# Evicting z at the scheduler's highest priority, and holding back the second unit's states by eight turns, in a hybrid encoder kernel

## The chip, the core and the metric

The kernel runs on one core of a Trainium2 chip. A core has a matrix engine (PE, with its weight loads listed as PEld), a vector engine (DVE), an activation engine (ACT), a general-purpose engine (POOL) and a queue engine (SP); ACT, POOL and SP also issue DMA transfers. Each engine works through its own list of instructions in order and waits on semaphores for the others. The metric is the device time of one execution in microseconds (us), lower being better.

## The reference, cut to what matters

Two layers, each a token-mixing and a channel-mixing part, on 512 tokens of 1024 channels in float32. The change lies in the token mixer, in the part that the reference calls `bidirectional_ssd` and in the gate z beside it:

```python
proj = x @ w_in
u_pool, z, xbc, dt_raw, gate_logits = jnp.split(proj, list(IN_SPLITS), axis=-1)
xbc = jax.nn.silu(dwconv_centred(xbc, ssd_conv_w, ssd_conv_b))     # width 5
xs, bm, cm = jnp.split(xbc, [SSD_INNER, SSD_INNER + gn], axis=-1)
y = bidirectional_ssd(xh, dt_raw, a_log, dt_bias, bm, cm, d_skip)
y = gated_rmsnorm(y, z, ssd_norm_g)                                # v = y * silu(z), ...

# inside ssd_scan, per direction, chunks of 128 tokens, 32 heads of 64 channels, 4 groups:
decay = jnp.exp(jnp.where(lower, seg, -jnp.inf))
scores = jnp.einsum('bclgn,bcsgn->bcgls', cc, bc)
y_diag = jnp.einsum('bcghls,bcsghp->bclghp', scores[:, :, :, None] * decay, x)
y_off = jnp.einsum('blgn,bghpn,bghl->blghp', c_c, h, jnp.exp(ac_c))
new_state = jnp.einsum('blgn,bghl,blghp->bghpn', b_c, decay_end, x_c)
h = h * jnp.exp(ac_c[..., -1])[..., None, None] + new_state
```

## The kernel before, in words

**Units and jobs.** The mixer of a layer `l` works on eight units `u`, of four heads each. `unit(u)` projects the unit's x (two tiles `xp`, 512 tokens wide) and z (two banks `zp`, two chunks each) in products of three matmuls (`mm3`: high times high, high times low, low times high; lines L385 to L387; the halves `wh` and `wl` of each block of weights are made by ACT at L96 and by DVE at L97). The big products are the steady work of PE. Everything else runs as background jobs. At fixed points between the big matmuls `bg.tick()` lets the jobs go on, at most one that does something in each turn; a job says with `yield n` for how many turns it rests. So the place of each small matmul among the big ones on PE is fixed when the program is written.

**A unit's steps**, with the names in the trace: conv of x on ACT (L477) and four taps on DVE (L483), Silu on ACT (L812) gives `xc`; `xt` transposes it on PE (L818), and ACT copies it to `xtok` (L952). POOL multiplies `xtok` into `xw` (L1061, two pieces) and into `y` (L1067, `dsk`). Three matmul pairs `stp` (L1078) make the states of three chunk borders, which ACT, POOL and DVE turn into `s` (L1084, L1086, L1093). `yop` (L1105) reads them; DVE scales the result to `yo` (L1111) and POOL adds it to `y` (L1119). At the end `zs * y` on DVE (L1124).

**Heads.** For each head `decay(h)` issues a DMA of 512 KB to a tile `m` from ACT's queue (L998; three buffers, so head h+3's transfer waits for head h's matmuls), POOL masks both halves (L1003, followed by a small DMA issue from POOL, L151), ACT takes eight exponentials (L1010), DVE adds the halves (L1012) and multiplies by the scores `sct` (L1022), and PE does the 16 small matmuls `ydp` (L1029), which DVE adds to `y` (L1035). Once per two units `btp` transposes B (L818) and `scp` makes the scores (L839); their input `bt` and the unit's `xc` share two buffers.

**What sets the order.** PE follows the program. On ACT, DVE and POOL a scheduler places the instructions by priority. ACT switches its function table (`ACT_TABLE_LOAD`) whenever an exponential follows a Silu or the other way round. z's eviction is an ACT Silu from a bank to `zs` (L978).

In the trace names carry no head or unit. In layer 0, the `xw` at 120 us is `xw_1`, the `stp` at 121.7 `stp_1_1`, the `ydp` at 104.2 `ydp_3`, at 127.2 `ydp_5`, the `scp` at 144.4 `scp_1`, the `xt` at 158.5 `xt_2_1`. In the listings of the order a name is tile, layer, unit or head, part and a running number: `m0_5_1115` is head 5's decay tile of layer 0, and `xt0_2_1` is unit 2's second transpose.

Of the kernel before, what the change touches and what calls it, by code (L numbers as in the profile page):

```python
# [12 lines left out]
AF = mybir.ActivationFunctionType  # L13
# [289 lines left out]
def tile_hybrid_pool_ssd_convffn_encoder(  # L303
# [24 lines left out]
    nc = tc.nc  # L328
# [8 lines left out]
    def bank_a(name):  # L337
        return psa.tile([P, 512], F32, tag="a", name=name)

    def bank_b(name):  # L340
        return psb.tile([P, 512], F32, tag="b", name=name)
# [40 lines left out]
    def mm3(ps, ah, al, bh, bl, first, last, resumed=False):  # L382

        mm = partial(nc.tensor.matmul, ps, skip_group_check=resumed)
        mm(lhsT=ah, rhs=bh, start=first, stop=False)  # L385
        mm(lhsT=ah, rhs=bl, start=False, stop=False)  # L386
        mm(lhsT=al, rhs=bh, start=False, stop=last)  # L387
# [43 lines left out]
    def feature_tiles(name, n):  # L431

        tiles = []
        for i in range(n):
            wh, wl = ws.get()
            ps = bank_a(f"{name}{i}")
            for k in range(KD):
                mm3(ps[: wh.shape[2], :], wh[:, k, :], wl[:, k, :], xts["h"][:, k, :],
                    xts["l"][:, k, :], k == 0, k == KD - 1)
                if k % 2:  # L440
                    bg.tick()
            tiles.append(ps)
        return tiles
# [333 lines left out]
    for l in range(NL):  # L777
# [31 lines left out]
        def conv_silu(ps, ft, name, tag="cv", bufs=2):  # L809
            cv = sp.tile([P, T], F32, tag=tag, name=name, bufs=bufs)  # L810
            conv(cv, ps, xbc_taps(ft), xbc_bias(ft))
            nc.scalar.activation(cv, cv, AF.Silu)  # L812
            return cv
# [137 lines left out]
        def x_job(u, i, cv, xtok):  # L951
            nc.scalar.copy(  # L952
                xtok[:, :, i * P : (i + 1) * P], transpose_tokens(cv, f"xt{l}_{u}_{i}")
            )
            yield 1

        def unit(u):
            nm = f"{l}_{u}"
            xtok = sp.tile([P, NCH, 256], F32, tag="xtok", name=f"xtok{nm}", bufs=2)
            xjobs = []  # L960
            for i in range(2):
                (xps,) = feature_tiles(f"xp{nm}_{i}_", 1)
                cv = conv_silu(xps, 2 * u + i, f"xc{nm}_{i}")
                xjobs.append(bg.spawn(x_job(u, i, cv, xtok), 11))
            zs = sp.tile([P, NCH, 256], F32, tag="zs", name=f"zs{nm}", bufs=3)
            wz = [ws.get() for _ in range(2)]
            for cc in range(2):
                ps = bank_a(f"zp{nm}_{cc}")
                for ci in range(2):
                    c = 2 * cc + ci  # L970
                    s = slice(c * P, (c + 1) * P)
                    for k in range(KD):
                        wh, wl = wz[k // 4]
                        mm3(ps[:, ci * 256 : (ci + 1) * 256], xts["h"][:, k, s], xts["l"][:, k, s],
                            wh[:, k % 4, :], wl[:, k % 4, :], k == 0, k == KD - 1)
                        if k % 4 == 3:
                            bg.tick()
                nc.scalar.activation(  # L978
                    zs[:, 2 * cc : 2 * cc + 2, :],
                    ps.rearrange("p (c n) -> p c n", c=2), AF.Silu,  # L980
                )

            return bg.spawn(unit_job(u, xtok, zs, xjobs), 1)

# [58 lines left out]
        def unit_job(u, xtok, zs, xjobs):  # L1043
            nm = f"{l}_{u}"
            g = u // 2
            while not (dts and g in grp and all(j.done for j in xjobs)):
                yield 0
            ct, btok, sct = grp[g]
            ef, nac, wst, tot = dts["ef"], dts["nac"], dts["wst"], dts["tot"]

            def hb(tile_, c0, c1, d, h0=4 * u, nh=4):
                return tile_[:, c0:c1, d * 32 + h0 : d * 32 + h0 + nh][:, :, :, None].broadcast_to(
                    [P, c1 - c0, nh, 64]
                )

            def h4(ap):
                return ap.rearrange("p c (h q) -> p c h q", q=64)

            xw = sp.tile([P, 2, 3, 256], F32, tag="xw", name=f"xw{nm}")
            for d in range(2):  # L1060
                nc.gpsimd.tensor_tensor(  # L1061
                    h4(xw[:, d]), h4(xtok[:, d : d + 3, :]), hb(wst, d, d + 3, d), op=ALU.mult
                )
            while u and u - 1 not in zst:
                yield 0
            y = sp.tile([P, NCH, 256], F32, tag="y", name=f"y{nm}")
            nc.gpsimd.tensor_tensor(  # L1067
                h4(y), h4(xtok),
                dsk[:, None, 4 * u : 4 * u + 4][:, :, :, None].broadcast_to([P, NCH, 4, 64]),
                op=ALU.mult,  # L1070
            )
            ytiles[u] = (xtok, y)
            yield 4
            st = {}
            for i in range(1, 4):
                ps = bank_b(f"stp{nm}_{i}")
                for d, c in ((0, i - 1), (1, 4 - i)):
                    nc.tensor.matmul(  # L1078
                        ps[:, d * 256 : (d + 1) * 256], lhsT=btok[:, c, :],
                        rhs=xw[:, d, c - d, :], start=True, stop=True,  # L1080
                    )
                s_new = sp.tile([P, 512], F32, tag="st", name=f"s{nm}_{i}", bufs=3)
                if i == 1:
                    nc.scalar.copy(s_new, ps)  # L1084
                else:
                    nc.gpsimd.tensor_tensor(  # L1086
                        s_new.rearrange("p (d h q) -> p d h q", d=2, q=64),
                        st[i - 1].rearrange("p (d h q) -> p d h q", d=2, q=64),
                        tot[:, i - 2, :, 4 * u : 4 * u + 4][:, :, :, None].broadcast_to(
                            [P, 2, 4, 64]),  # L1090
                        op=ALU.mult,
                    )
                    nc.vector.tensor_tensor(s_new, s_new, ps, op=ALU.add)  # L1093
                st[i] = s_new
                yield 1

            yield 4
            for c in (1, 2, 0, 3):
                ps = bank_b(f"yop{nm}_{c}")
                yo = sp.tile([P, 2, 256], F32, tag="yo", name=f"yo{nm}_{c}", bufs=2)  # L1100
                for d in range(2):
                    i = c if d == 0 else 3 - c
                    if i == 0:
                        continue
                    nc.tensor.matmul(  # L1105
                        ps[:, d * 256 : (d + 1) * 256], lhsT=ct[:, c * P : (c + 1) * P],
                        rhs=st[i][:, d * 256 : (d + 1) * 256], start=True, stop=True,
                    )
                d0, d1 = (1 if c == 0 else 0), (1 if c == 3 else 2)
                efv = ef[:, c, :].rearrange("p (d h) -> p d h", d=2)  # L1110
                nc.vector.tensor_tensor(  # L1111
                    yo[:, d0:d1].rearrange("p d (h q) -> p d h q", q=64),
                    ps.rearrange("p (d h q) -> p d h q", d=2, q=64)[:, d0:d1],
                    efv[:, d0:d1, 4 * u : 4 * u + 4][:, :, :, None].broadcast_to(
                        [P, d1 - d0, 4, 64]),
                    op=ALU.mult,
                )
                for d in range(d0, d1):
                    nc.gpsimd.tensor_tensor(y[:, c, :], y[:, c, :], yo[:, d, :], op=ALU.add)  # L1119
                yield 1  # L1120

            while heads_done[0] < 4 * u + 4:
                yield 0
            nc.vector.tensor_tensor(zs, zs, y, op=ALU.mult)  # L1124
            zst[u] = zs
            if u % 2:
                yield from norm(g, *new_yt(g))
# [56 lines left out]
        def new_yt(g):  # L1184
            pool = accp
            yts[g] = (
                pool.tile([P, 4, T], F32R, tag="yth", name=f"yth{l}_{g}"),
                pool.tile([P, 4, T], F32R, tag="ytl", name=f"ytl{l}_{g}"),
            )
            return yts[g]  # L1190
# [247 lines left out]
```

## Time and profile before

| | |
|---|---|
| median of 3 runs | 1984.68 us (1984.16 to 1985.37) |
| profiled execution | 1980.59 us, span from first to last instruction 1978.9 us |
| mean granted TensorE clock | 0.993 |
| PE busy | 1928.7 us (97%) |
| DVE, ACT, POOL busy | 65%, 50%, 29% |

PE is the engine that is hardly ever idle, so time is read as the idle stretches of PE, what ended each, and how fast PE ran behind it. A busy share of PE says little of how fast its clock was; the granted clock does.

### The profile page before, as it was taken

How to read it: one execution, taken by the hardware profiler on the slowest of the kernel's cores; microseconds unless marked ns; L12 is line 12 of the kernel's file. 1: busy time of each engine (PE TensorE's matmuls, PEld its weight loads, DVE VectorE, ACT ScalarE, POOL GpSimd, SP SyncE). 2: the span in 40 equal slices, each digit the busy share in tenths (PEclk: the TensorE clock that was granted, in tenths of full speed). 3: DMA queues.
4: the chain of work that ended last, by engine and by line, in shares of the span. 5: the costliest groups of instructions: out<-in, count | busy, mean ns of one | idle time of the engine just before them, and what ended most of it. 6: DMA issues, size and time to landing. Idle time of an engine off the chain costs nothing.

```text
span 1978.9 us, 27549 instructions
## 1 busy us (share of the span) xinstructions
PE 1928.7 (97%) x10449; PEld 1618.0 (82%) x10449; DVE 1279.8 (65%) x1945; ACT 996.1 (50%) x1665; POOL 578.6 (29%) x698
## 2 busy tenths in 40 slices
PE   8999999999999999999999999999999999999997
PEld 7877898888888888887888878988888888888786
DVE  5568575766556666665785685757665576666577
ACT  4767665654332434444457675656443334444453
POOL 1344525252021233320004445242421113333201
PEclk9999999999999999999999999999999999999999
DMA  5554536353233567767536545363532417677763
GB/s 160 147 145 144 155 91 150 107 128 124 91 103 116 165 186 181 187 211 269 158 109 177 146 125 142 108 165 96 144 107 75 156 58 201 182 193 188 251 229 108
DMA packets 204996, 295.65 MB, mean 149 GB/s; under 512 B 11424, under 2 KB 132420, under 8 KB 204864
## 3 DMA queue, kind: packets, MB, share of 16 engines
q1 hardware_dynamic: 160976, 187.45, 29.6%
q0 software_dynamic: 26176, 72.36, 15.2%
q10 hardware_dynamic: 17712, 34.08, 6.8%
q8 instruction: 83, 1.36, 0.3%
q14 instruction: 49, 0.40, 0.1%
HBM read 280.75 MB, written 59.24 MB: 172 GB/s over the span
## 4 chain that ended last, share of the span: by engine, by line
PE 77%; issue 8%; DMA 5%; DVE 4%; ACT 3%; POOL 2%; ACTq 0%; POOLq 0%; DVEq 0%; SPq 0%
PE fg L386 7%; PE fg L385 7%; PE fg L387 7%; DMA m<-acd 3%; PE spp L385 3%; PE spp L386 3%; PE spp L387 3%; PE zp L385 2%; PE zp L386 2%; PE zp L387 2%; PE stp L1078 2%; PE xp L385 2%; PE xp L387 2%; PE xp L386 2%; PE ydp L1029 2%
## 5 line engine op out<-in xcount | busy, mean ns | idle before, releaser
L97 DVE TENSOR_TENSOR wl<-wraw,wh 128x1024 fp32r<-128x1024 f32 (+1 forms) x346 | 424.8, 1229 | 296.5 <-ACT wh L96 295.0
L96 ACT CAST wh<-wraw 128x1024 fp32r<-128x1024 f32 (+1 forms) x346 | 355.2, 1028 | 484.1 <-PE fg L386 92.4
L387 PE MATMUL fg<-xthm,wl 128*128 128x512 f32 x640 | 249.0, 389 | 0.0
L385 PE MATMUL fg<-xthm,wh 128*128 128x512 f32 x640 | 249.0, 389 | 0.0
L386 PE MATMUL fg<-xtlm,wh 128*128 128x512 f32 x640 | 249.0, 389 | 0.0
L1010 ACT ACTIVATE m<-m,nac 128x128 f32<-128x128 f32 x512 | 158.8, 390 | 69.5 <-POOL m L1003 69.0
L1003 POOL TENSOR_SCALAR_AFFINE_SELECT m<-m 128x512 f32<-128x512 f32 x128 | 96.5, 778 | 180.4 <-DMA m<-acd 150.7
L385 PEld LDWEIGHTS fg<-xthm,wh 128*128 128x128 f32 x640 | 120.2, 188 | 24.9
L387 PEld LDWEIGHTS fg<-xthm,wl 128*128 128x128 f32 x640 | 120.2, 188 | 24.9
L386 PEld LDWEIGHTS fg<-xtlm,wh 128*128 128x128 f32 x640 | 120.2, 188 | 24.9
L1119 POOL TENSOR_TENSOR y<-y,yo 128x256 f32<-128x256 f32 x96 | 84.3, 889 | 90.5 <-DVE yo L1111 88.0
L385 PE MATMUL spp<-yth,wh 128*128 128x512 f32 x256 | 110.3, 431 | 0.5 <-ACT yth L1159 0.5
L1012 DVE TENSOR_TENSOR m<-m 128x512 f32<-128x512 f32 x64 | 46.6, 729 | 88.0 <-ACT m L1010 75.9
L386 PE MATMUL spp<-ytl,wh 128*128 128x512 f32 x256 | 101.2, 395 | 0.7 <-DVE ytl L1160 0.7
L387 PE MATMUL spp<-yth,wl 128*128 128x512 f32 x256 | 101.0, 395 | 0.0
L483 DVE SCALAR_TENSOR_TENSOR xc<-xp,pcwc,xc 128x510 f32<-128x510 f32 (+1 forms) x128 | 95.1, 745 | 5.3 <-ACT xc L477 3.7
L567 POOL TENSOR_TENSOR x<-x,lnb 128x512 f32<-128x512 f32 x15 | 22.4, 1500 | 240.6 <-DVE x L563 240.6
L1061 POOL TENSOR_TENSOR xw<-xtok,wst 128x768 f32<-128x768 f32 x32 | 50.6, 1600 | 115.3 <-ACT xtok L952 93.6
L385 PE MATMUL zp<-wh,xthi 128*128 128x256 f32 x256 | 77.2, 302 | 0.0
L385 PE MATMUL zp<-wh,xthf 128*128 128x256 f32 x256 | 77.1, 301 | 0.0
L1296 POOL TENSOR_TENSOR g<-g,acc 128x512 f32<-128x512 f32 x16 | 27.8, 1740 | 161.9 <-ACT g L1257 150.2
L386 PE MATMUL zp<-wl,xthi 128*128 128x256 f32 x256 | 72.9, 285 | 0.9 <-DVE wl L97 0.9
(399 smaller groups left out, 5143.8 us busy)
## 6 DMA issues: line engine op xcount, KB each, us to landing
wraw<-in_w_in_dram SPq DMA_DIRECT2D x56, 1024.0 KB, 5.6
wraw<-in_w_up_dram SPq DMA_DIRECT2D x44, 1024.0 KB, 6.6
t<-in_w_down_dram POOLq DMA_DIRECT2D x132, 256.0 KB, 4.7
m<-acd ACTq DMA_DIRECT2D x64, 512.0 KB, 5.8
wraw<-in_w_ssd_proj_dram SPq DMA_DIRECT2D x16, 1024.0 KB, 5.1
wraw<-t SPq DMA_DIRECT2D x32, 512.0 KB, 4.8
wraw<-in_w_down_dram SPq DMA_DIRECT2D x46, 256.0 KB, 3.4
t<-t POOLq DMA_DIRECT2D x44, 256.0 KB, 5.6
```

The source lines that it names most:

```text
L96: self.nc.scalar.copy(hv, src)
L97: self.nc.vector.tensor_tensor(lv, src, hv, op=ALU.subtract)
L385: mm(lhsT=ah, rhs=bh, start=first, stop=False)
L386: mm(lhsT=ah, rhs=bl, start=False, stop=False)
L387: mm(lhsT=al, rhs=bh, start=False, stop=last)
L483: nc.vector.scalar_tensor_tensor(dst[:, o0:o1], ps[:, o0 + s : o1 + s], tap, dst[:, o0:o1], op0=ALU.mult, op1=ALU.add,)
L1003: mask = nc.gpsimd.affine_select(out=mv, in_=mv, pattern=[[0, NCH], [1 - 2 * d, P]], compare_op=ALU.is_ge, fill=NEG, base=0, channel_multi ...
L1010: nc.scalar.activation(mc, mc, AF.Exp, bias=nac[:, c, col : col + 1])
L1012: nc.vector.tensor_tensor(m[:, 0], m[:, 0], m[:, 1], op=ALU.add)
L1029: nc.tensor.matmul(ps[q * 64 : (q + 1) * 64, c * 64 : (c + 1) * 64], lhsT=m[:, 0, t0 : t0 + 64], rhs=xtok[:, c, hh * 64 : (hh + 1) * 64], ...
L1061: nc.gpsimd.tensor_tensor(h4(xw[:, d]), h4(xtok[:, d : d + 3, :]), hb(wst, d, d + 3, d), op=ALU.mult)
L1119: nc.gpsimd.tensor_tensor(y[:, c, :], y[:, c, :], yo[:, d, :], op=ALU.add)
```

## The change

z's eviction is placed with the highest priority, and the job of unit 1 alone rests eight turns instead of four between `y` and its first `stp`.

```diff
-                nc.scalar.activation(
-                    zs[:, 2 * cc : 2 * cc + 2, :],
-                    ps.rearrange("p (c n) -> p c n", c=2), AF.Silu,
-                )
+                with tc.high_priority():
+                    nc.scalar.activation(
+                        zs[:, 2 * cc : 2 * cc + 2, :],
+                        ps.rearrange("p (c n) -> p c n", c=2), AF.Silu,
+                    )
@@ unit_job
             ytiles[u] = (xtok, y)
-            yield 4
+            yield 8 if u == 1 else 4
             st = {}
             for i in range(1, 4):
                 ps = bank_b(f"stp{nm}_{i}")
```

All lines behind L978 stand one lower in the changed file. PE's list keeps its 8849 rows and SP's order is the same. ACT's list grows from 1250 to 1258 rows, by eight table loads (85 to 93, four in each layer); DVE's and POOL's are cut into a few rows more. Both layers are changed alike.

**First place: ACT, layer 0, around the weight cast `wh15`**, a half of z's weights for unit 2; `m0_3`, `m0_4` and `m0_5` are the decays of heads 3 to 5.

```order
-L1010 ACT_TABLE_LOAD
-L1010 ACTIVATE m0_3_1003<-m0_3_1003,nac0_717 128x128 x6
+L999 DMA m0_4_1056<-acd0_95 128x2x512
+L999 DMA m0_5_1115<-acd0_95 128x2x512
 L96 CAST wh15_1157<-wraw8_1155 128x1024
-L1010 ACTIVATE m0_3_1003<-m0_3_1003,nac0_717 128x128 x2
-L1010 ACTIVATE m0_4_1056<-m0_4_1056,nac0_717 128x128 x8
-L998 DMA m0_5_1115<-acd0_95 128x2x512
+L1011 ACT_TABLE_LOAD
+L1011 ACTIVATE m0_3_1003<-m0_3_1003,nac0_717 128x128 x8
+L1011 ACTIVATE m0_4_1056<-m0_4_1056,nac0_717 128x128 x8
```

The table load and the first six exponentials of head 3 stood ahead of the cast; now the load and all eight stand behind it.

**Second place: PE inside z's product of unit 2, and DVE a little later.** On PE, where unit 1's first states stood:

```order
 L386 MATMUL zp0_2_0_1298<-wl15_1158,xthi_100 128x256
 L387 MATMUL zp0_2_0_1298<-wh15_1157,xtli_101 128x256
-L1078 MATMUL stp0_1_1_1364<-xw0_1_1262,btok0_0_574 128x256 x2
+L818 MATMUL btp0_1_1365<-ident_66,bt0_1_1140 128x128 x4
 L385 MATMUL zp0_2_0_1298<-wh16_1238,xthi_100 128x256
 L386 MATMUL zp0_2_0_1298<-wl16_1239,xthi_100 128x256
```

The transpose of B for the next group takes their place; the three `stp` now stand where `stp_1_2` and `stp_1_3` stood and behind `ydp_7`. On DVE, before, head 5's product by the scores (the last step ahead of `ydp_5`) stands ahead of `zs * y` of unit 0:

```order
L1111 TENSOR_TENSOR yo0_0_0_1216<-yop0_0_0_1215,ef0_712 128x256
L1111 TENSOR_TENSOR yo0_0_3_1227<-yop0_0_3_1226,ef0_712 128x256
L1022 TENSOR_TENSOR m0_5_1115<-m0_5_1115,sct0_0_598 128x512
L1124 TENSOR_TENSOR zs0_0_538<-zs0_0_538,y0_0_838 128x1024
L97 TENSOR_TENSOR wl17_1291<-wraw9_1288,wh17_1290 128x1024
```

And with the change:

```order
L1125 TENSOR_TENSOR zs0_0_538<-zs0_0_538,y0_0_838 128x1024
L97 TENSOR_TENSOR wl17_1291<-wraw9_1288,wh17_1290 128x1024
L483 SCALAR_TENSOR_TENSOR xc0_2_0_1231<-xp0_2_0_0_1161,pcwc_149,xc0_2_0_1231 128x511
L1036 TENSOR_TENSOR y0_1_1265<-y0_1_1265,ydp0_4_1311 128x4x64
L483 SCALAR_TENSOR_TENSOR xc0_2_0_1231<-xp0_2_0_0_1161,pcwc_149,xc0_2_0_1231 128x511
L1013 TENSOR_TENSOR m0_6_1191<-m0_6_1191 128x512
L483 SCALAR_TENSOR_TENSOR xc0_2_0_1231<-xp0_2_0_0_1161,pcwc_149,xc0_2_0_1231 128x510
L1023 TENSOR_TENSOR m0_5_1115<-m0_5_1115,sct0_0_598 128x512
```

Head 5's product has moved behind `zs * y` of unit 0, behind the addition to unit 1's `y`, and behind head 6's sum. On POOL the masks of `m0_6` and both pieces of `xw0_1` now stand ahead of the last two additions to `y0_0`, and `y0_1`, which uses the buffer of `y0_0`, behind `zs * y`.

**Third place: PE in unit 3's second x tile, and ACT at that time.** On PE unit 2's second transpose comes in the place of unit 1's first `yop`:

```order
 L387 MATMUL xp0_3_1_0_1580<-xthi_100,wl18_1295 128x512
-L1105 MATMUL yop0_1_1_1612<-s0_1_1_1367,ct0_0_423 128x256
-L1105 MATMUL yop0_1_1_1612<-s0_1_2_1439,ct0_0_423 128x256
+L818 MATMUL xt0_2_1_1612<-ident_66,xc0_2_1_1280 128x128 x4
 L385 MATMUL xp0_3_1_0_1580<-xthi_100,wh18_1294 128x512
```

The transpose stood some 10 us later, behind z's first bank; ahead of it on PE are now `scp_1`, six matmuls, `xt_2_0` and six more. On ACT the instructions that lead to it now read:

```order
L999 DMA m0_9_1465<-acd0_95 128x2x512
L96 CAST wh20_1576<-wraw10_1498 128x1024
L999 DMA m0_10_1533<-acd0_95 128x2x512
L477 ACTIVATE xc0_2_1_1280<-xp0_2_1_0_1242,pcbc_151,pcwc_149 128x512
L1011 ACTIVATE m0_9_1465<-m0_9_1465,nac0_717 128x128 x8
L1011 ACTIVATE m0_10_1533<-m0_10_1533,nac0_717 128x128 x6
L812 ACT_TABLE_LOAD
L812 ACTIVATE xc0_2_1_1280<-xc0_2_1_1280 128x512
```

Before, head 10's exponentials stood behind the Silu of `xc0_2_1`, and head 9's ahead of its conv; the table load for the Silu was paid for z's second bank just ahead. The conv of `xc0_2_1` waits for `scp_1`, whose `bt` had its buffer.

## Rows read from the trace of the kernel before

**Rows 1.** PE's waits: waiter, releaser, us in total, times, longest.

```profile
PE stp L1078 <- POOL xw L1061: 6.3, 4, 2.0
...
PE g0p L385 <- ACT zs L978: 4.3, 2, 2.3
```

**Rows 2.** PE's timeline at the states, layer 0: start, duration, instruction, [idle, releaser].

```profile
119.49 0.28 PE L387 MATMUL zp<-wh,xtli 128*128 128x256 f32 x1
...
127.21 0.69 PE L1029 MATMUL ydp<-xtok,m 128*64 128x64 f32 x16
...
130.79 1.02 PE L1078 MATMUL stp<-xw,btok 128*128 128x256 f32 x4
...
133.18 0.69 PE L1029 MATMUL ydp<-xtok,m 128*64 128x64 f32 x16
```

**Rows 3.** The same place in layer 1.

```profile
1102.03 0.28 PE L387 MATMUL zp<-wh,xtlf 128*128 128x256 f32 x1
...
1109.44 0.94 PE L1029 MATMUL ydp<-xtok,m 128*64 128x64 f32 x16
```

**Rows 4.** A window behind the states: stretch, length, PE busy, granted clock, DMA share, GB/s.

```profile
124.20:127.20 3.00, 3.00 (x14) 0.53 0.00 0
```

**Rows 5.** ACT's timeline: a table load, and the cast `wh15` with what follows.

```profile
82.10 0.60 ACT L978 ACTIVATE zs<-zp 128x512 f32<-128x512 f32 x1
82.71 1.28 ACT L1010 ACT_TABLE_LOAD   x1
84.01 0.40 ACT L1010 ACTIVATE m<-m,nac 128x128 f32<-128x128 f32 x1
...
99.97 1.05 ACT L96 CAST wh<-wraw 128x1024 fp32r<-128x1024 f32 x1 [3.11 <-PE bc L386]
100.93 3.03 ACT L1010 ACTIVATE m<-m,nac 128x128 f32<-128x128 f32 x10
```

**Rows 6.** PE at `ydp_3`, and DVE's two steps for head 3.

```profile
104.19 0.69 PE L1029 MATMUL ydp<-xtok,m 128*64 128x64 f32 x16 [0.39 <-ACT m L1010]
...
102.20 0.69 DVE L1012 TENSOR_TENSOR m<-m 128x512 f32<-128x512 f32 x1
103.41 0.68 DVE L1022 TENSOR_TENSOR m<-m,sct 128x512 f32<-128x512 f32 x1
```

**Rows 7.** POOL's and DVE's steps around `xw_1`.

```profile
107.14 1.23 POOL L1003 TENSOR_SCALAR_AFFINE_SELECT m<-m 128x512 f32<-128x512 f32 x2 [1.33 <-DMA m<-acd]
114.11 1.89 POOL L1119 TENSOR_TENSOR y<-y,yo 128x256 f32<-128x256 f32 x2 [1.43 <-DVE yo L1111]
120.21 3.35 POOL L1061 TENSOR_TENSOR xw<-xtok,wst 128x768 f32<-128x768 f32 x2 [4.21 <-ACT xtok L952]
123.52 1.89 POOL L1067 TENSOR_TENSOR y<-xtok,dsk 128x1024 f32<-128x1024 f32 x1
...
116.03 1.23 DVE L1124 TENSOR_TENSOR zs<-zs,y 128x1024 f32<-128x1024 f32 x1 [0.63 <-POOL y L1119]
125.44 0.42 DVE L1035 TENSOR_TENSOR y<-y,ydp 128x256 f32<-128x256 f32 x1 [1.77 <-POOL y L1067]
```

**Rows 8.** The decay tiles `m` from 90 to 160 us: their transfers.

```profile
DMA to landing us min/median/max: 4.5/6.1/7.9
```

**Rows 9.** PE around `scp_1`, from `btp_1` to the first `yop`.

```profile
142.55 0.60 PE L818 MATMUL btp<-ident,bt 128*128 128x128 f32 x4
142.90 0.48 PE L385 MATMUL xp<-xthi,wh 128*128 128x512 f32 x1
...
144.39 1.05 PE L839 MATMUL scp<-ct,bt 128*128 128x128 f32 x8
...
148.47 0.38 PE L1105 MATMUL yop<-s,ct 128*128 128x256 f32 x1
```

**Rows 10.** ACT and DVE on `xc_2_1`: conv and three taps.

```profile
149.41 0.77 ACT L477 ACTIVATE xc<-xp,pcbc,pcwc 128x512 f32<-128x512 f32 x1
...
150.21 2.32 DVE L483 SCALAR_TENSOR_TENSOR xc<-xp,pcwc,xc 128x510 f32<-128x510 f32 x3 [1.83 <-ACT xc L477]
```

## Prediction, made before the changed kernel ran

> **What bounds the kernel now.** The page shows PE busy for nearly the whole span, so I read PE's list of waits first: what PE waited for, how long, and how often. The reader should see that POOL's `xw` holding up the states `stp` is the largest of all, 6.3 us in four waits, two in each layer [rows 1]. Then I read PE's timeline at that place. In layer 0 the last matmul of z's half product starts at 119.49 and its successor could start 0.12 later (the pitch of these matmuls), at 119.61; PE reaches the next `ydp` only at 127.21, 7.60 us on [rows 2]. The same work, a pair of `stp` and twelve matmuls, takes 2.39 us where nothing waits, from 130.79 to 133.18 [rows 2]. So this place costs 5.2 us in layer 0, and by the same subtraction 1109.44 - 1102.15 - 2.39 = 4.9 us in layer 1 [rows 3]. That is more than the idle time of 3.15 us a layer: behind the waits the granted clock stood at 0.53 for 3 us, the lower of its two levels (1.2 of 2.4 GHz) [rows 4], which loses 3.0 x 0.47 = 1.4 us. So a stall of some 2 us has a price of its own behind it, and I carry that to the new stalls below.
>
> Last I read ACT, DVE and POOL at the three places where the order moves, for what PE will find late there.
>
> **The change, part by part.**
>
> *The states, delayed.* `xw_1` is late because ACT copies the second half of `xtok_1` behind six exponentials of head 6; POOL's two pieces end 3.35 us after 120.21 [rows 7]. With the change `stp_1_1` comes after `ydp_5` and two dozen more matmuls, near 130 us, and POOL has the pieces ready near 118 (below). The wait goes and so does the slow clock behind it: -5.2 in layer 0, -4.9 in layer 1. `btp_1`, which takes the place at about 121.7, needs only `bt`, whose Silu stands on ACT behind three exponentials of head 6 and a load; with that head's masks done at 114.3 (below) it is there near 117, so it costs nothing but itself.
>
> *Eight more table loads.* 8 x 1.28 = 10 us of ACT, which idles half the time: nothing by themselves. They count where a chain towards PE runs through one.
> The Trainium skill, "ScalarE: Activation LUTs", section "What ACT_TABLE_LOAD costs", speaks against this part of the change: a switch of set is a load of 1283 ns and a drain of about 1380 ns, and calls should be grouped by set. The trace agrees on the load and shows no drain: Silu ends at 82.70, the load runs from 82.71 to 83.99, the exponential starts at 84.01 [rows 5]. By the page's price each of the two chains below with a load on it (`ydp_3` and `xt_2_1`) would be 1.4 us longer, an estimate of 5.5 us more in all; I go by the row.
>
> *`ydp_3`.* Head 3's eight exponentials now all stand behind the cast `wh15`, which PE releases and which ends at 101.02 [rows 5]. Table load 1.28, then eight at a pitch of 0.29 (ten took 3.03 [rows 5]): 104.7. DVE's sum and product, 0.69 and 0.68 [rows 6]: 106.1, with the handover 106.2. Before, `ydp_3` started at 104.19 after waiting 0.39 [rows 6]. So +2.0. Whether the clock falls behind a stall of about 2.4 us I leave to the range: 0 to 1.4.
>
> *`ydp_5`.* All of PE is now 2.0 later. PE would be ready for `ydp_5` at 119.61 + 2.0 + 2.1 = 123.7 (a transpose is 0.3 shorter than a pair of `stp` [rows 2, 9]). But head 5's product on DVE now stands behind unit 1's `y` and head 6's sum. The chain: `ydp_3` ends at 106.9 and releases head 6's transfer, at 107.0; it lands 6.1 later (4.5 to 7.9 [rows 8]), at 113.1. From there POOL: masks 1.23, `xw_1` 3.35, two additions to `y_0` 1.89; DVE `zs * y` 1.23; POOL `y_1` 1.89; DVE addition 0.42, two taps of 0.77, sum and product of 0.7 each [rows 6, 7, 10]. That is 12.95 us, so 126.1. Stall 2.4; with the fastest and slowest transfer 0.8 and 4.2. For the clock I take half the price, 0.7.
>
> *`xt_2_1`.* Let T be the end of unit 3's first x tile (142.55 before). PE's work from T to the transpose is what lay between 142.90 and 148.47, 5.57 us [rows 9]. `scp_1` starts at T + 1.49 and ends at T + 2.54 [rows 9]; only then can ACT write the conv of `xc_2_1` (0.77), then four taps of 0.77 with head 9's sum (0.65) between them [rows 6, 10], then a table load 1.28, then Silu 0.60 [rows 5]: T + 9.1 with handovers, so at least 3.5 us too late. On ACT there is more ahead of that load: head 10's transfer is issued behind the cast `wh20`, which waits for T; landing 6.1 later, masks 1.23, two exponentials 0.7, load, Silu: T + 10.05. Stall 4.5 (3.5 by the floor, 6.3 with a transfer of 7.9), and 1.4 for the clock. Before, the transpose stood 10 us later and waited for nothing.
>
> *The rest.* PE's wait of `g0p` for z's bank is 4.3 us [rows 1], and an earlier eviction would end it, but `zs_3` does not move in ACT's order: it still stands behind the exponentials of heads 12 and 13, so I give nothing. The other moved evictions lead to no PE row that had less than some microseconds to spare; at nothing, too. If that cover is gone, one is worth a table load and a Silu, 1.9 us.
>
> *Sum.* Per layer +2.0, +2.4 + 0.7, +4.5 + 1.4 = +11.0, against -5.2 and -4.9: +5.8 and +6.1, together +11.9. On the profiled execution, 1980.59, that gives 1992.5. The median of the runs is 4.1 higher, so I add the sum to it: 1984.68 + 11.9 = 1996.6. Low end: the three terms at their floors without clock, 2.0 + 0.8 + 3.5 = 6.3 a layer, +2.5, 1987.2. High end: 2.0 + 4.2 + 6.3 + 3 x 1.4 = 16.7 a layer, +23.3, 2008.0.
>
> **The rivals.**
>
> *A. The delay is partly given back at `g0p`.* PE comes to `g0p` later, and if ACT's exponentials there do not come later with it, the 4.3 us of waiting and a slow clock behind each of the two (2 x 1.4) go: 11.9 - 7.1 = +4.8, 1989.5. Against it: head 11's transfer there is released by `ydp_8`, so the chain moves along with PE. For it: parts of the chain are transfers whose length varies by 3.4 us [rows 8].
>
> *B. The decays run early, and the change gains.* The two stalls at `ydp_3` and `ydp_5`, and what exceeds the bare chain of `xc_2_1`, all hang on exponentials being late on ACT. If ACT is not held up where I think (transfers and exponentials done before PE asks), only the bare chain of `xt_2_1` stays, without head 9's sum: 3.5 - 0.65 = 2.8 a layer. Then -10.1 + 5.6 = -4.5, 1980.2. It decides for a gain once all three new stalls together are under 3.0 us a layer. Against it: head 3's eight exponentials can't start before the cast, whose start PE sets.
>
> *C. Slow transfers.* All at 7.9 with the clock falling behind each stall: the high end, 2008.
>
> *D. The states still wait,* since `xw_1` now stands behind head 6's masks on POOL: it would have to come 10 us later than I place it; then the -10.1 is missing, and the time is over 2005.
>
> **How the numbers follow.** My sum 0.63, A 0.17, B 0.11, C 0.08, D 0.01. The time is that of the sum, 1996.6, its own range 1987 to 2008. From A's lower part, 1984, to 2005 leaves out B and C's outer part, under 2 in 10. A measurement can tell about 0.2%, 4 us, from no change: below 1980.7 lies B, 0.11; up to 1988.7 lie the floor of my sum and half of A, 0.15; the rest is slower, 0.74.
>
> **What would show it.** In the new trace PE's waits should have no `stp <- xw` of 2 us at unit 1, but `ydp` waiting for head 3 and head 5 by 2 to 3 us each, and a transpose `xt` waiting for ACT's Silu of `xc` by 4 to 5, once in each layer, with granted clock near 0.5 behind the last. `xw_1` should end near 118. I am wrong if that transpose doesn't wait 3 us, or if PE's list of waits is shorter in sum than before.

## The result and the profile after

The changed kernel takes 2000.78 us in the median of four runs (1997.79 to 2005.81), the kernel before 1984.42 in four runs beside them (1981.32 to 1985.37): a ratio of 1.0088, 95% interval 1.0072 to 1.0103, or 14 to 20 us more. It is slower, inside the range of the prediction and 4 us above its figure. Timed again later in twelve runs (below, experiment 9) it took 1993.82 us, ratio 1.0047 (1.0033 to 1.0060), 3 us below the figure. Both timings are used in what follows; most of their difference goes with TensorE's granted clock (experiment 9).

The page of the profiled execution, the slowest of the first four (2005.81 us), and its clock:

```profile
span 2004.0 us, 27539 instructions
PE 1938.6 (97%) x10449; PEld 1625.4 (81%) x10449; DVE 1278.0 (64%) x1945; ACT 1007.1 (50%) x1673; POOL 576.1 (29%) x698
core 0: 2004.0 us, clock 0.986
```

The busy shares are within a point of those of before; beside the span only the clock (0.993 before) says that something is off. PE's waits in the changed kernel say what:

```profile
PE xt L818 <- ACT xc L812: 9.6, 2, 5.6
PE dp_v L385 <- ACT wh L96: 8.0, 2, 4.4
...
PE ydp L1030 <- DVE m L1023: 5.5, 2, 2.8
...
PE ydp L1030 <- POOL m L1004: 3.7, 1, 3.7
...
PE ydp L1030 <- issue: 1.8, 1, 1.8
...
PE g0p L385 <- ACT zs L979: 0.9, 2, 0.8
```

The row of `stp` waiting for `xw`, 6.3 us [rows 1], is gone. In its place stand `ydp` (5.5 for `ydp_3`; 3.7 and 1.8 for `ydp_5`, to which the list gives POOL's masks in layer 0 and nothing in layer 1; in both, PE starts 0.1 us behind the end of DVE's product of head 5, below) and the transpose `xt` (9.6). The wait of `g0p` for z has fallen from 4.3 us [rows 1] to 0.9. The wait of `dp_v`, which lies outside the token mixer, was 4.7 before; in the experiments it varies between 3.8 and 8.1 whatever the kernel (8.1 in experiment 6, which costs nothing; 3.8 in experiment 9, the changed kernel again). So it belongs to the execution and not to the change, but it weighs when two executions are compared (experiment 9).

PE's timeline in layer 0 of the changed kernel, in order `ydp_3`, `ydp_4`, `ydp_5`, the first `stp` of unit 1, `ydp_6`, `scp_1`, `xt_2_1` and the first `yop` of unit 1:

```profile
107.49 1.12 PE L1030 MATMUL ydp<-xtok,m 128*64 128x64 f32 x16 [2.75 <-DVE m L1023]
...
122.12 0.69 PE L1030 MATMUL ydp<-xtok,m 128*64 128x64 f32 x16
131.43 1.13 PE L1030 MATMUL ydp<-xtok,m 128*64 128x64 f32 x16 [3.68 <-POOL m L1004]
137.69 1.02 PE L1079 MATMUL stp<-xw,btok 128*128 128x256 f32 x4
140.06 0.69 PE L1030 MATMUL ydp<-xtok,m 128*64 128x64 f32 x16
...
151.70 1.05 PE L839 MATMUL scp<-ct,bt 128*128 128x128 f32 x8
...
161.59 1.12 PE L818 MATMUL xt<-ident,xc 128*128 128x128 f32 x4 [5.60 <-ACT xc L812]
...
164.99 1.02 PE L1106 MATMUL yop<-s,ct 128*128 128x256 f32 x4
```

Three stalls, at the three places that the prediction named. Each is followed by slow matmuls: a `ydp` group of 16 takes 1.12 instead of 0.69 [rows 2]. The windows behind them, and last the stretch where the clock was low before [rows 4] (stretch, length, busy time of PE, PEld, DVE, ACT, POOL, then granted clock, DMA share, GB/s):

```profile
110.20:113.20 3.00, 3.00 (x8) 2.34 (x8) 0.84 (x2) 3.00 (x9) 2.03 (x4) 0.50 0.48 128
133.40:136.40 3.00, 3.00 (x16) 3.00 (x16) 0.00 (x0) 2.99 (x8) 0.00 (x0) 0.50 0.16 44
161.60:164.60 3.00, 3.00 (x9) 2.57 (x10) 0.96 (x2) 2.99 (x6) 0.00 (x0) 0.50 0.00 0
124.00:127.00 3.00, 3.00 (x28) 3.00 (x27) 2.80 (x3) 2.08 (x6) 1.92 (x1) 1.00 0.48 120
```

The clock has its lower level (1.2 of 2.4 GHz) behind each new stall of this layer, and its full one where it was low before. One stall with its slow stretch has been traded for three.

ACT in the changed kernel at the first and the third place:

```profile
100.91 1.05 ACT L96 CAST wh<-wraw 128x1024 fp32r<-128x1024 f32 x1 [3.78 <-PE bc L386]
101.98 1.28 ACT L1011 ACT_TABLE_LOAD   x1
103.28 4.78 ACT L1011 ACTIVATE m<-m,nac 128x128 f32<-128x128 f32 x16
...
110.40 0.37 ACTq L999 DMA_DIRECT2D m<-acd  x1
...
150.34 0.37 ACTq L999 DMA_DIRECT2D m<-acd  x1
152.80 0.78 ACT L477 ACTIVATE xc<-xp,pcbc,pcwc 128x512 f32<-128x512 f32 x1 [1.46 <-PE scp L839]
...
157.74 1.86 ACT L1011 ACTIVATE m<-m,nac 128x128 f32<-128x128 f32 x6 [1.82 <-POOL m L1004]
159.62 1.28 ACT L812 ACT_TABLE_LOAD   x1
160.91 0.63 ACT L812 ACTIVATE xc<-xc 128x512 f32<-128x512 f32 x1
```

At `ydp_3` the chain is as predicted: cast, table load, eight exponentials, then DVE. At `xt_2_1` PE waits for the Silu that ends at 161.54; ahead of it on ACT stand a table load and six exponentials of head 10, and these wait for POOL's masks and so for the transfer that ACT issued at 150.34.

POOL in the changed kernel: the masks of head 6, `xw_1` and `y_1`; behind them DVE, from the addition to `y_1` to the products of heads 5 and 6.

```profile
116.77 2.21 POOL L1004 TENSOR_SCALAR_AFFINE_SELECT m<-m 128x512 f32<-128x512 f32 x2 [4.44 <-PE xt L818]
...
119.47 2.91 POOL L1062 TENSOR_TENSOR xw<-xtok,wst 128x768 f32<-128x768 f32 x2
...
125.08 2.81 POOL L1068 TENSOR_TENSOR y<-xtok,dsk 128x1024 f32<-128x1024 f32 x1 [1.34 <-DVE zs L1125]
```

```profile
127.92 0.42 DVE L1036 TENSOR_TENSOR y<-y,ydp 128x256 f32<-128x256 f32 x1 [1.12 <-POOL y L1068]
...
130.65 1.28 DVE L1023 TENSOR_TENSOR m<-m,sct 128x512 f32<-128x512 f32 x2
```

`xw_1` ends at 122.4, and the first `stp` comes at 137.69: it has 15 us to spare. Head 5's product starts at 130.65 and takes 0.68 [rows 6], so it ends at 131.3, and `ydp_5` starts at 131.43: the chain behind head 6's masks, through `y_1` and the addition to it, is the one that the prediction named.

### The profile page after: what moved, and what is told of

It is laid out like the page before. It is cut to its first block, busy times and chain, and to the rows that moved or that the text cites. A ratio compares the mean times of both kernels' runs of the same rounds, so it can differ in the third digit from the quotient of the medians.

```text
span 2004.0 us, 27539 instructions
## 1 busy us (share of the span) xinstructions
PE 1938.6 (97%) x10449; PEld 1625.4 (81%) x10449; DVE 1278.0 (64%) x1945; ACT 1007.1 (50%) x1673; POOL 576.1 (29%) x698
## 4 chain that ended last, share of the span: by engine, by line
PE 75%; issue 8%; DMA 6%; DVE 5%; ACT 3%; POOL 2%; POOLq 0%; ACTq 0%; DVEq 0%; SPq 0%
PE fg L385 7%; PE fg L386 7%; PE fg L387 7%; DMA m<-acd 4%; PE spp L385 3%; PE spp L386 3%; PE spp L387 3%; PE zp L385 3%; PE zp L386 2%; PE zp L387 2%; PE xp L385 2%; PE xp L386 2%; PE xp L387 2%; PE yop L1106 2%; PE stp L1079 2%
## 5 line engine op out<-in xcount | busy, mean ns | idle before, releaser
L97 DVE TENSOR_TENSOR wl<-wraw,wh 128x1024 fp32r<-128x1024 f32 (+1 forms) x346 | 432.1, 1250 | 305.3 <-ACT wh L96 303.9
```

The lines of the kernel that those rows point to most:

```text
L97: self.nc.vector.tensor_tensor(lv, src, hv, op=ALU.subtract)
```

## The experiments

Times in brackets beside each are the kernel before, on the same chip. Experiments 1 to 4, 5 to 7, 8, and 9 and 10 ran in one go each. "A stretch" is the time from the start of one PE instruction to the start of another, in the profiled execution of the kernel named.

**1. The eight turns alone.**

```diff
-            yield 4
+            yield 8 if u == 1 else 4
```

> Only the eight turns, z's eviction without priority. My account: the waits of the states go (-10 us in two layers), ydp_3 and ydp_5 do not wait, since ACT and DVE keep their old order up to there, but xt_2_1 comes early as in the whole change and waits 4 to 6 us in each layer, with 1.4 us or more of slow clock behind it: -10 + 12 = about +2 us, less what is given back at g0p (up to 7), so between -5 and +3 against before. Rival (the delay is a plain gain, and the priority costs it all): -10 us, 1974.

Measured: 1985.65 us in 11 runs (1984.89 in 29), ratio 1.0008 (0.9997 to 1.0019). No change, within the -5 to +3 that was expected; the rival's -10 is out. From `ydp_4` to `ydp_5`, where the states stood, PE takes 5.55 us in both layers (11.19 and 10.88 before), which is 5.6 and 5.3 less; 0.3 of each is that a transpose stands there in the place of a pair of `stp`. What takes it back, in PE's waits:

```profile
PE xt L818 <- ACT xc L812: 6.9, 2, 3.4
...
PE yop L1105 <- DVE yo L1111: 2.8, 1, 2.8
...
PE ydp L1029 <- DVE m L1022: 2.5, 2, 1.4
```

The transpose `xt_2_1` waits 3.4 us with no priority in play: the bare chain from `scp_1` through conv, taps, load and Silu, which the prediction put at 3.5. `ydp_3` waits for nothing new (6.29 us from `ydp_2`, as before).

**2. The priority alone.**

```diff
+                with tc.high_priority():
                     nc.scalar.activation(
...
```

> Only the priority, four turns as before. My account: ydp_3 waits 2 us more and ydp_5 some 3 to 5 us for head 5's product, in each layer, with slow clock behind them; the states hardly wait, since PE comes later to them and POOL has xw_1 earlier; xt_2_1 stands late and does not wait: +8 to +12 us. Rival (the priority alone carries the whole loss): +25 us. Other rival (evictions are harmless by themselves): within 2 us.

Measured: 1989.29 us in 12 runs (1984.89), ratio 1.0022 (1.0011 to 1.0033): slower, by 4.4 us, less than expected. In its waits:

```profile
PE ydp L1030 <- DVE m L1023: 8.2, 3, 3.1
...
PE ydp L1030 <- ACT m L1011: 3.3, 1, 3.3
```

`ydp_3` and `ydp_5` wait in both layers. There is no wait of unit 1's `stp` left either, as expected: PE, held up at `ydp_3`, comes to it at 126.72, and `xw_1` ended at 121.94. The stretches of the table below come to +9.0 us in this profiled execution (1993.61 us) and to +3.7 in that of experiment 7 (1984.18), where the priority also stands for units 1 and 2: `ydp_3` and `ydp_5` wait nearly as long in both (11.5 and 11.0), but the slow clock behind them costs 5.3 more here. So this execution lies in the expected +8 to +12, and the median below it; that other executions pay less for the clock, as experiment 7's does, is likely and not shown.

**3. The whole change, with `xt_2_1` held back** (its job rests 16 turns instead of 11).

```diff
-                xjobs.append(bg.spawn(x_job(u, i, cv, xtok), 11))
+                xjobs.append(bg.spawn(x_job(u, i, cv, xtok), 16 if (u, i) == (2, 1) else 11))
```

> The whole change, but unit 2's second transpose is spawned 16 turns on instead of 11, which puts it behind unit 1's four yop on PE (and lets head 8 and what follows stand up to one turn later). My account: the wait of xt_2_1 and the slow clock behind it go, 2 x 6 us less than the whole change, so about +4 us against before; some of the g0p wait comes back, so up to +9. Rival (the wait only moves to the next thing that ACT owes, so nothing is won): +16.

Measured: 1993.3 us in 5 runs (1984.89), ratio 1.0049 (1.0037 to 1.0061), about +9.7, a little over the +4 to +9 that was expected. The transpose waits no more, but `g0p` does, 7.5 us instead of 0.9:

```profile
PE g0p L385 <- ACT zs L979: 7.5, 2, 3.9
```

**4. The eight turns alone, with `xt_2_1` held back** in the same way.

> The eight turns without priority, and the transpose late as in the run before. My account: only the gain of the states stays, -10 us, with the g0p waits as before: 1973 to 1977. Rival (the states' wait only passes on to the next late thing): within 3 us of before.

Measured: 1987.9 us in 11 runs (1984.89), ratio 1.0016 (1.0006 to 1.0027). No gain, where 1973 to 1977 was expected: the rival was right.

```profile
PE g0p L385 <- ACT zs L978: 7.4, 2, 3.8
...
PE xt L818 <- ACT xc L812: 4.0, 2, 2.2
```

Holding a job back also holds back what follows it in turn, and the waits appear at `g0p` and at the next transpose.

**5. The eight turns, with three turns instead of four ahead of unit 1's `yop`.** From the first `yop` on, PE's places are then those of the kernel before.

```diff
-            yield 4
+            yield 8 if u == 1 else 4
...
-            yield 4
+            yield 3 if u == 1 else 4
```

> Eight turns without priority, and unit 1 rests three turns instead of four between its states and its yop. That puts every matmul from unit 1's first yop on where it stood before the change, the transpose xt_2_1 too; of the change only the later states and the earlier btp stay. If the run with the late transpose lost its gain only because head 8 and what follows stood a turn later, this one keeps it: -11 for the states, +3 for ydp_7 as in the run with eight turns alone, so -8 us or about 1977. If the wait of the states passes on in any case, it shows again at g0p (4 us a layer instead of 2) and the time is within 3 us of before.

Measured: 1981.51 us in 11 runs (1984.03 in 25), ratio 0.9992 (0.9981 to 1.0003): not to be told from no change, where about 1977 was hoped for. The 5.6 and 5.3 us at the states stay gained. But now the next transpose, `xt_3_0`, waits:

```profile
PE xt L818 <- ACT xc L812: 9.7, 2, 5.4
```

**6. The priority for all units but 1 and 2.**

```diff
+                with tc.high_priority() if u not in (1, 2) else ExitStack():
```

> Priority alone, for all units but 1 and 2. My account: the priority costs by what it does to ACT's order around heads 3 to 6, which is units 1 and 2; for the other units it is worth nothing: within 2 us of before, ydp_3 and ydp_5 as before. Rival (each of the eight added table loads has its price): most of the +4 of the run with priority alone.

Measured: 1983.38 us in 12 runs (1984.03), ratio 0.9994 (0.9985 to 1.0004). `stp` and `g0p` wait as in [rows 1], 6.5 and 4.0 us. No effect, as expected. But ACT loads its table 85 times in this run, as before the change, and 93 times in experiments 2 and 7: none of the eight added loads is in it, so it doesn't test the rival that each of them has a price.

**7. The priority for units 1 and 2 alone** (`u in (1, 2)`).

> Priority alone, for units 1 and 2 only. My account: all of the +4 us of the run with priority alone, with ydp_3 waiting 3 us and ydp_5 2 to 3 us in each layer, and the states not waiting. Rival: about +1.

Measured: 1990.23 us in 8 runs (1984.03), ratio 1.0030 (1.0020 to 1.0041). `ydp` waits 11.0 us in four. These two units carry the priority's loss, +6.0 (4.0 to 8.1) against +4.4 (2.2 to 6.6) in experiment 2.

**8. Experiment 5, with the priority given to the conv and the Silu of `xc_3_0`,** so that `xt_3_0` needn't wait.

```diff
-            conv(cv, ps, xbc_taps(ft), xbc_bias(ft))
-            nc.scalar.activation(cv, cv, AF.Silu)
+            with tc.high_priority() if name.endswith("_3_0") else ExitStack():
+                conv(cv, ps, xbc_taps(ft), xbc_bias(ft))
+                nc.scalar.activation(cv, cv, AF.Silu)
```

> The kernel before with the eight turns for unit 1's states, three turns instead of four before its read-outs (as in the run with yop at three turns), and the scheduler's priority for the eviction and Silu of xc_l_3_0 alone. The theory (the gain of the states, 5.5 us a layer, was kept there and then lost at xt_3_0, which waited 4.5 to 5.5 us a layer for the Silu of xc_3_0 behind head decays on ScalarE): that wait falls below 1 us, so the time comes 8 to 12 us under the kernel before; some 2 us a layer may return where g0p waits for the gated z, which leaves -5 to -12 us, 1972 to 1979 us. The rival (what is taken off TensorE's path comes back at the next place where ScalarE is late, whatever is moved): the decays of the heads that are pushed back, or g0p, take the wait over, and the time is within 3 us of before; the waits of ydp or g0p then sum to 8 us or more over the two layers.

Measured: 1993.87 us in 6 runs (1984.67 in 10), ratio 1.0040 (1.0024 to 1.0055). My theory fell: `xt_3_0` waits for nothing, and its median is 12 us over that of experiment 5. The rival was right in kind, too mild in size:

```profile
PE stp L1079 <- POOL xw L1062: 5.9, 4, 1.9
PE g0p L385 <- ACT zs L979: 4.8, 2, 2.8
PE g0p L385 <- ACT u L1203: 4.0, 2, 2.3
```

ACT switches its table four times between 149.5 and 156.8 us, two times more than there in experiment 5, in each layer. The copy of unit 2's second `xtok`, at 160.70 in experiment 5 and ahead of the next table load and Silu, now stands behind them at 169.05; so POOL's `xw` is late, and so are the states of unit 2. ACT, POOL and PE there:

```profile
169.05 1.07 ACT L953 COPY xtok<-xt 128x512 f32<-128x512 f32 x2
```

```profile
169.71 3.82 POOL L1062 TENSOR_TENSOR xw<-xtok,wst 128x768 f32<-128x768 f32 x2 [11.20 <-ACT xtok L953]
```

```profile
172.10 0.70 PE L1079 MATMUL stp<-xw,btok 128*128 128x256 f32 x2 [1.89 <-POOL xw L1062]
```

It is the kind of wait that the change was to take from unit 1, one unit on: from `ydp_8` to `ydp_9` PE takes 10.3 and 10.4 us instead of 5.8 before. How much of the delay is the added loads and how much the order on ACT was not separated.

**9. The whole change again,** unchanged.

> The whole change once more, beside the next kernel and with more runs of the kernel before. The two parts alone measured +1.6 and +4.4 us, the whole +17.4. If the parts hinder each other (the place of xt_2_1 costs more when ScalarE is late by the priority as well): the time stays at +14 to +20 us, 1998 to 2004, and the wait of xt for the Silu of xc is above 8 us in its two. If the first figure was an accident of few runs and the parts merely add: +5 to +9 us, 1989 to 1993.

Measured: 1993.82 us in 12 runs (1984.22 in 22), ratio 1.0047 (1.0033 to 1.0060). The whole costs 9.3 us here, the two parts alone 1.6 + 4.4: at most a few us are left for the parts hindering each other, and the intervals don't settle these. The wait of `xt` is 8.0:

```profile
PE xt L818 <- ACT xc L812: 8.0, 2, 4.0
...
PE ydp L1030 <- DVE m L1023: 5.5, 2, 2.8
PE ydp L1030 <- POOL m L1004: 5.1, 2, 3.0
```

The mixer's stalls are those of the first profile to within 1.6 us each. The two profiled executions, 1985.4 and 2004.0 us, differ by 11.0 us in how long PE is busy with the same work (1927.6 and 1938.6), which is the clock, and by 7.6 in its idle time. Of the idle time 4.2 lies at `dp_v` (3.8 against 8.0), where ACT's cast waits for a transfer of weights, 5.90 and 4.68 us here and 7.37 and 7.31 there; with the clock behind it, the 61 matmuls from there on take 7.3 us less here, in the two layers together. Over the twelve runs the time goes from 1985.63 us at a mean granted clock of 0.993 to 1997.95 at 0.987, with a mean of 0.990, and the first four stand at 0.986 to 0.989, with a mean of 0.987. Of 1990 us, 0.003 is 6 us, and the medians are 7.0 apart. Why the clock stayed low longer in the first four is open; the record doesn't name their chip.

**10. The whole change, with three turns ahead of unit 1's `yop`,** as in experiment 5.

> The whole change with three turns instead of four ahead of unit 1's read-outs, so that TensorE's places from the first yop on are those of the kernel before and xt_2_1 does not move up. The theory of the prediction (the stalls at ydp_3 and ydp_5 and the one at xt_2_1 are separate terms, the last some 6 us a layer): without xt_2_1's stall the time comes 8 us or more below the whole change. Since the eight turns alone with this edit kept a stall of 5 us a layer at xt_3_0 in place of that at xt_2_1, the rival is that the same happens here, the wait of xt for xc is again 8 us or more in two, and the time is within 4 us of the whole change.

Measured: 1987.22 us in 12 runs (1984.22), ratio 1.0009 (0.9995 to 1.0023); 6.6 us below experiment 9, between the 8 of the theory and the 4 of the rival. The waits side with the theory:

```profile
PE xt L818 <- ACT xc L812: 2.9, 2, 1.4
...
PE g0p L385 <- ACT zs L979: 2.4, 2, 1.3
```

From `scp_1` to `xt_3_0` PE takes 4.1 us less in each layer than in experiment 9; at `g0p` it gives back 1.3 and 0.8. That makes -6.2. In this execution `ydp_3` with the clock behind it costs 3.3 us more than in experiment 9's, so that all the stretches of the table below come to 2.7 less, and the two profiled spans are alike (1985.5 and 1985.4, one of the fastest of experiment 9's twelve). The 6.6 us are the medians' and not the profiles'.

## Why the prediction was right, and where its sum was off

The terms against the stretches in which they lie, in us (before, after, experiment 9):

| stretch on PE | term | layer 0 | layer 1 |
|---|---|---|---|
| `ydp_2` to `ydp_3` | +2.0 | 6.28, 8.65, 8.65 | 6.29, 8.65, 8.65 |
| `ydp_3` to `ydp_4` (clock) | 0 | 11.83, 14.63, 13.28 | 11.83, 13.36, 13.36 |
| `ydp_4` to `ydp_6` (states, `ydp_5`) | -2.1, -1.8 | 17.16, 17.95, 14.63 | 17.11, 13.41, 15.07 |
| `ydp_7` to `scp_1` | 0 | 5.32, 5.75, 5.75 | 5.32, 5.75, 5.75 |
| `scp_1` to `xt_3_0` | +5.9 | 18.88, 25.92, 24.29 | 18.61, 25.17, 24.31 |
| `ydp_11` to `ydp_12` (`g0p`) | 0 | 32.84, 30.01, 29.57 | 33.01, 30.61, 29.75 |
| sum of the differences | +5.8, +6.1 | after +10.6, exp. 9 +3.9 | after +4.8, exp. 9 +4.7 |

Experiment 9's sum, +8.6, stands against +6.5 for the span of its profiled execution, a fast one, and +9.3 for the medians. The first profile's, +15.4, leaves 9.7 us of its span's excess outside these rows, in an execution at the slow end of its runs; 6.4 of these lie at `dp_v` and in the slow clock behind it, where experiment 9 takes 0.9 less than the kernel before. From `ydp_7` to `scp_1` a pair of `stp` stands in the place of the transpose; the 0.4 is that work.

*The states: right.* The wait is gone, with the slow clock behind it, and `xw_1` is ready in time, so rival D is out. From `ydp_4` to `ydp_6` the gain is 5.6 in both layers (experiment 1); less the 0.4 of moved work that is 5.2, where I had 5.2 and 4.9.

*`ydp_3`: right.* +2.4 for +2.0, by the chain named: cast ends at 101.96, load to 103.26, exponentials from 103.28. The Trainium skill, "ScalarE: Activation LUTs", section "What ACT_TABLE_LOAD costs", adds a drain of about 1380 ns to the load; here the first exponential again follows the load within 0.02 us, so the trace disagrees with the drain, as it did before the change.

*The clock behind `ydp_3`: the term that I left out.* I left it to the range, 0 to 1.4 a layer, and took 0. It cost 1.5 (three of the four layers) or 2.8.

*`ydp_5`: right in sum.* 3.1 predicted with the clock; experiment 9 has 14.63 - 11.52 = 3.1 in layer 0 and 3.6 in layer 1, where 11.52 is 5.55 + 5.97 from experiment 1. The first profile has 6.4 and 1.9. The chain was longer than I had it: the transfer of head 6 was issued at 110.40, not at 107.0, since PE was later and the issue stands on ACT behind exponentials of head 5. So `xw_1` ended at 122.4 and not near 118, with no effect. PE was later too, by the clock, so that the stall stayed near its size.

*`xt_2_1`: right.* Predicted to wait 4.5; it waited 5.6 and 4.0, in experiment 9 4.0 twice. Its stretch grew by 5.4 and 5.7 in experiment 9, and by 7.0 and 6.6 in the first profile, for 5.9. Experiment 10 takes the place away and 6.6 us with it.

*`g0p`: the step that failed.* I gave it nothing, because `zs_3` does not move on ACT, and set against rival A that "head 11's transfer there is released by `ydp_8`, so the chain moves along with PE". Before the change it was not `ydp_8` that held this transfer:

```profile
167.56 0.63 ACT L812 ACTIVATE xc<-xc 128x512 f32<-128x512 f32 x1 [1.31 <-DVE xc L483]
167.65 0.37 ACTq L998 DMA_DIRECT2D m<-acd  x1
```

`ydp_8` ended at 165.91, and the issue came 1.7 us later, since on ACT's list it stands behind a Silu that waited for DVE. In the changed kernel the three stalls lie ahead of `ydp_8` on PE and bring it 14.4 us later, that Silu only 7.7 (it ends at 175.9):

```profile
179.68 1.05 ACT L96 CAST wh<-wraw 128x1024 fp32r<-128x1024 f32 x1 [0.33 <-PE zp L387]
180.30 0.37 ACTq L999 DMA_DIRECT2D m<-acd  x1
```

Here `ydp_8` ends at 180.26 and the transfer goes out at once. From the start of `ydp_8` to `zs_3` it takes 23.0 and 23.5 us instead of 25.5 and 25.3 (22.9 and 22.7 in experiment 9): the chain moved along with PE only in part. The wait fell from 4.3 to 0.9, in experiment 9 to nothing, and the stretch by 3.3 a layer in experiment 9 (2.8 and 2.4 in the first profile). So what rival A named, at 0.17, came true, and its -7.1 measured -6.5 and -5.2; its time, 1989.5, lies under both timings, since it left out the clock as I did. In experiment 10, with `xt_2_1`'s stall gone, the transfer goes out as early, but `zs_3` comes 24.1 and 23.8 us behind `ydp_8` and `g0p` waits 2.4 again; on what this last microsecond hangs isn't shown. The two errors, +3.0 to +4.3 of clock and -5.2 to -6.5 at `g0p` that were left out, cancel in part: that the figure stands between the two timings, 4 and 3 us from them, is in part luck.

*Priority against turns.* Units 1 and 2 carry the priority's loss (experiments 6 and 7), by `ydp_3` and `ydp_5`. The turns gain 11 us at the states and lose as much at `xt_2_1` and the waits beside it (experiment 1).

*The other rivals.* B would have needed the three new stalls together under 3.0 us a layer; they are 12.0 and 8.6 in the first profile. C's stalls of 4.2 and 6.3 with all transfers slow were not reached: 3.7 and 5.6 are the longest seen.

*No better kernel.* Five attempts to keep the gain (experiments 3, 4, 5, 8, 10) ended, by their ratios, between 1.6 us under and 9.7 us over the kernel before; the best, experiment 5, can't be told from it. Each time a wait came back at a later PE instruction whose input passes through ACT: `xt_2_1`, `xt_3_0`, `g0p`, `stp`; experiments 3 and 10 also keep the priority's waits of `ydp`. That ACT's order in the mixer is the limit, though it is busy for half of the span, fits all ten runs; a run in which ACT is given less work was not made, so it is argued and not shown. The same chains pass through the heads' transfers and POOL's masks ahead of ACT, and no run changes these alone.

## What to carry to other kernels

A stall on the busy engine that is removed comes back at the next place where another engine has nothing to spare, so look up how early each later input is before counting the gain. When a new stall is put ahead of an old wait, check what really holds the start of the old wait's chain, and not only what could release it: if another engine's list holds it, the chain does not move along with the stall, and the old wait shrinks. And a higher priority for an instruction on a switching engine can cost what is queued behind it a table load and its turn: with units 1 and 2 it did, with the other six it cost neither a load nor time (experiments 6 and 7).

## What had not been expected of the hardware

The slow clock behind a stall has two prices. From `ydp_3` to `ydp_4` PE takes 11.83 us wherever `ydp_3` waited 0.4 us or nothing new (before and experiments 1, 4, 5, 6, 8). Where it waited 2.7 us or more, in six runs and both layers, the stretch takes 13.3 to 13.4 us six times and 14.3 to 14.7 us six times, and nothing between. The same kernel has both: 14.63 and 13.36 in the two layers of the first profile, behind the same stall of 2.75 us. Behind `ydp_5` the price can also be none: in experiment 9 PE takes 5.98 us from `ydp_5` to `ydp_6` behind a wait of 3.03 us and 7.43 behind one of 2.02, where 5.97 is the time with no stall (experiment 1). In these runs the length of a stall of 2 to 3 us does not tell its price.
